# Two edits to a hybrid decoder trunk: the matmuls of two inversion levels issued together in the first mixer's recurrence, and two tiles of gate-and-up allocated in another order

## The chip, the cores and the metric

The kernel runs on one core of a Trainium2 chip. The metric is the device time of one execution in microseconds (us), the median of three runs. The engines are named as in the profile: PE does matmuls, PEld its weight loads, DVE, ACT and POOL are the vector, scalar and GpSimd engines, SP issues the DMAs. L987 is line 987 of the kernel. PSUM, into which PE writes, has banks of 128x512 float32 values.

## The reference

Two layers over 1024 tokens of width 1024, in float32. Cut to the parts that the change touches:

```python
def mixer_ab(h, ...):                     # layer 0
    qkv, z, beta_raw, alpha_raw, gate_b, gate_c, sc_in = split_cols(h @ w_in, AB_SPLITS)
    ...
    o_a = gated_delta_rule(q, k, v, g, beta)
    o_a = rms_norm(o_a, norm_g) * silu(z)
    o_b = gate_b * causal_depthwise_conv(gate_c * sc_in, sc_conv_w)
    return concatenate([o_a, o_b]) @ w_out

def gated_delta_rule(q, k, v, g, beta):   # chunkwise
    ...
    sol = triangular_solve(a_strict + eye(c), rhs, lower=True, unit_diagonal=True)
    ...                                   # then a scan over the chunks with a state per head

def swiglu(h, w_gate, w_up, w_down):      # after the mixer of each layer
    return (silu(h @ w_gate) * (h @ w_up)) @ w_down
```

The mixer of layer 1 (HGRN2 and dilated window attention) is not touched.

## The kernel before, in words

Activations lie transposed in two halves of 512 tokens. A product in float32 is made of three fp32r matmuls on split operands (`mm3`, L123 to L125): every weight tile arrives by DMA as `raw` and is split by an ACT cast (L99) and a DVE subtraction (L100) into a unit `w`.

**The recurrence of layer 0** (`delta`, in `mixer_ab`). Its 1024 tokens are eight chunks of 128. The inverse of each chunk's triangular matrix is built from 32x32 blocks in levels. `level1` and `level2` (matmuls at L971 and L987, 32x32 tiles) make the off-diagonal blocks of the 64x64 triangles; `level3` and `level4` (L999 and L1008, 64x64 tiles) make those of the 128x128 triangle. Each level writes its matmuls into one part of a PSUM bank of the kind `psg` (two buffers) and a reader takes them out: DVE L975 (`z1`), DVE L990 (a block of `yt`), ACT L1002 (`z2`), DVE L1009 (a block of `yt`). After L1009 DVE makes `y2` and `y1` (L1013, L1015). Levels of different chunks share a bank: in one step `level4` of chunk c+1 and `level2` of chunk c+2 write into `la`, in the next `level3` of chunk c+2 and `level1` of chunk c+3 write into `lb`. The columns are disjoint, but an access of one engine to a bank is ordered against another engine's access to the same bank, so matmuls into a bank wait for a reader of it that stands ahead of them in the program. Around the levels stand `values` (L1030, L1032), `state` (L1045, whose DVE part is L1049), `level5` (L1021), `outputs` (L1059, L1061) and `gated` (L1085).

`delta` is a generator. `short_conv` runs the projections of the short convolution and, after each half projection (12 matmuls of 128x512), calls `tick`, which runs `delta` up to its next `yield`. PE's order in this stage is the order of the program (`manual_schedule`); the order of DVE, ACT, POOL and SP is laid out by a planner, which starts from the program's order.

**Gate and up** (`Up`, once per layer). A product of 2x2 blocks is done with seven block products, `p1`, `p2`, `p5`, `p6`, `p7` and two in `end`, of 12 matmuls each for one of 22 column groups f. `turn` opens it while the second half's norm is still being made; there the order of PE, DVE, ACT and POOL is as written. It closes the trunk pool, which held the four 8 KB tiles a0, b0, a1, b1 (two halves by two quarters of the residual h), and opens the pool `up` over the same memory (`close()` and `self.right = right("up")`, L505 and L506). In `up` a tile takes its place in the order of first allocation: two weight units of 8 KB (`take`), four `hid` buffers of 2 KB, four kept buffers `kr` of 2 KB (`kept`), a pad. A tile waits for what last used its memory. The last uses are, in DVE's written order: a1 by the low part `t3l` (`rest(t3, a1)`), b0 by `t4l`, b1 by `b22l`; a0 last in the subtraction ahead of `t4l`. `p7` copies its bank into a kept tile (ACT L362, tile `c`) and adds another bank on DVE (L363). `end` first runs the product `a22` into the same bank as `p7` (tiles `t4h`, `t4l`), then `s4` (`b22h`, `b22l`), then DVE L372 and L377, ACT L378, POOL L379 and two DMAs.

Of the kernel before, what the change touches and what calls it, by code (L numbers as in the profile page):

```python
# [52 lines left out]
def hybrid_trunk_kernel(ctx: ExitStack, tc: tile.TileContext, x_t, w_all, w_four, w_down, w_ba, vecs, c_f, c_i, c_rope, out):  # L53
# [33 lines left out]
    def psg():  # L87
        return ps.tile([P, HT], F32, tag="g", name="psg", bufs=2)
# [160 lines left out]
    class Up:  # L249
# [160 lines left out]
        def turn(self, tr, row, b11, b21, hx, close, left, right):  # L410
# [57 lines left out]
            g = [self.snap(0)]  # L468
# [35 lines left out]
            rest(b22, b1)  # L504
            close()  # L505
            self.right = right("up")  # L506
            us = [self.take(), self.take()]
            self.first = [self.hidden()]
            self.p7(0, t3)
            self.right.tile([P, 32], F32, name="pad")  # L510
            self.p7(1, t3)
            self.add11(1, g[1])
# [111 lines left out]
    def mixer_ab(hn, rb, hp, close):  # L624
# [15 lines left out]
        with ExitStack() as es:  # L640
# [309 lines left out]
            def delta(yd, xd, load_al, load_cx):  # L950
# [4 lines left out]
                def hb(ap):  # L955
                    return ap[:, :, None].to_broadcast([P, 4, P])

                def bt(tag, shape=None, bufs=2):
                    return bp.tile([P] + (shape or [4, P]), F32, tag=tag, name=tag, bufs=bufs)
# [4 lines left out]
                ys, y2s, z1s, z2s, wts, us, sts, os_all, uu = {}, {}, {}, {}, {}, {}, {0: None}, {}, {}  # L964


                def level1(c, lv):
                    yt, x64, e0 = yts[c % 2], x64s[c % 2], c * 4
                    for h in range(4):
                        for r in (0, 64):  # L970
                            T.matmul(lv[r:r + 32, h * 32:(h + 1) * 32], als[c][r + 32:r + 64, h, r:r + 32],  # L971
                                     yd[r + 32:r + 64, e0 + h, :], start=True, stop=True)
                    z1 = z1s[c] = bt("z1", [4, 32])
                    for r in (0, 64):
                        V.tensor_copy(z1[r:r + 32], lv[r:r + 32, 0:P].rearrange("p (h t) -> p h t", h=4))  # L975
                    for b in range(4):
                        G.tensor_copy(yt[b * 32:(b + 1) * 32, :, b * 32:(b + 1) * 32],
                                      yd[b * 32:(b + 1) * 32, e0:e0 + 4, :])
                    for b in range(2):
                        G.tensor_copy(x64[b * 32:(b + 1) * 32, :, b * 32:(b + 1) * 32],  # L980
                                      xd[b * 32:(b + 1) * 32, e0:e0 + 4, :])

                def level2(c, lv):
                    yt, x64, z1 = yts[c % 2], x64s[c % 2], z1s.pop(c)
                    for h in range(4):
                        for r in (0, 64):
                            T.matmul(lv[r:r + 32, 256 + h * 32:256 + (h + 1) * 32], xd[r:r + 32, c * 4 + h, :],  # L987
                                     z1[r:r + 32, h, :], start=True, stop=True)
                    for r in (0, 64):
                        V.tensor_scalar(yt[r:r + 32, :, r + 32:r + 64],  # L990
                                        lv[r:r + 32, 256:256 + P].rearrange("p (h t) -> p h t", h=4),
                                        -1.0, None, op0=MULT)
                    for h in range(4):
                        V.transpose(x64[32:64, h, 0:32], yt[0:32, h, 32:64])

                def level3(c, lv):
                    al, yt = als.pop(c), yts[c % 2]
                    for h in range(4):
                        T.matmul(lv[0:64, 256 + h * 64:256 + (h + 1) * 64], al[64:128, h, 0:64],  # L999
                                 yt[64:128, h, 64:128], start=True, stop=True)  # L1000
                    z2 = z2s[c] = bp.tile([64, 4, 64], F32, tag="z2", name="z2", bufs=1)
                    S.copy(z2, lv[0:64, 256:512].rearrange("p (h t) -> p h t", h=4))  # L1002
                    load_al(c + 3)

                def level4(c, lv):
                    yt, x64, z2 = yts[c % 2], x64s[c % 2], z2s.pop(c)
                    for h in range(4):
                        T.matmul(lv[0:64, h * 64:(h + 1) * 64], x64[:, h, :], z2[:, h, :], start=True, stop=True)  # L1008
                    V.tensor_scalar(yt[0:64, :, 64:128], lv[0:64, 0:256].rearrange("p (h t) -> p h t", h=4),  # L1009
                                    -1.0, None, op0=MULT)  # L1010
                    if c:
                        y2 = y2s[c] = bt("y2", bufs=1)
                        V.tensor_tensor(y2, yt, hb(sca["c2"][:, c, :]), op=MULT)  # L1013
                    ys[c] = bt("y1")
                    V.tensor_tensor(ys[c], yt, hb(sca["c1"][:, c, :]), op=MULT)  # L1015

                def level5(c):
                    cx, y2 = cxs[c], y2s.pop(c)
                    o = psg()
                    for h in range(4):  # L1020
                        T.matmul(o[:, h * P:(h + 1) * P], cx[:, h, 0:P], y2[:, h, :], start=True, stop=True)  # L1021
                    wts[c] = bt("wt")
                    S.copy(wts[c], v4(o))

                def values(c):

                    cx, sp_ = cxs[c], sts[c]
                    pu = psm()
                    for h in range(4):
                        T.matmul(pu[:, h * P:(h + 1) * P], ys[c][:, h, :], cx[:, h, P:2 * P], start=True, stop=c == 0)  # L1030
                        if c:
                            T.matmul(pu[:, h * P:(h + 1) * P], wts[c][:, h, :], sp_[:, h, :], start=False, stop=True)  # L1032
                    u2 = None
                    if c < 7:
                        u2 = bt("u2", bufs=1)
                        V.tensor_tensor(u2, v4(pu), hb(sca["cu"][:, c, :]), op=MULT)
                    u = bt("u", bufs=1)
                    S.copy(u, v4(pu))
                    uu[c] = u, u2

                def state(c):
                    cx, sp_, u2 = cxs[c], sts[c], uu[c][1]
                    p2 = psm()
                    for h in range(4):
                        T.matmul(p2[:, h * P:(h + 1) * P], cx[:, h, 0:P], u2[:, h, :], start=True, stop=True)  # L1045
                    sn = sts[c + 1] = bt("st")
                    if c:
                        for h in range(4):
                            V.scalar_tensor_tensor(sn[:, h, :], sp_[:, h, :], sca["gt"][:, c, h:h + 1],  # L1049
                                                   p2[:, h * P:(h + 1) * P], op0=MULT, op1=ADD)  # L1050
                    else:
                        V.tensor_copy(sn, v4(p2))
# [17 lines left out]
                def gated(c):  # L1070
# [18 lines left out]
                    V.scalar_tensor_tensor(go, v4(o), vec[:, R_DNG:R_DNG + 1], szc, op0=MULT, op1=MULT)  # L1089
                    dma(catd[half][0:4, :, cc * P:(cc + 1) * P].rearrange("k p t -> p k t"), go)  # L1090

                for c in range(-3, 8):
                    if c > -3:
                        if c >= 0:
                            values(c)
                        la = psg() if c < 7 else None
                        if 0 <= c + 1 < 8:
                            level4(c + 1, la)
                        if 0 <= c + 2 < 8:
                            level2(c + 2, la)  # L1100
                        yield
                    if 0 <= c < 7:
                        state(c)
                    lb = psg() if c < 6 else None
                    if 0 <= c + 2 < 8:
                        level3(c + 2, lb)
                    if 0 <= c + 3 < 8:
                        level1(c + 3, lb)
                    if 1 <= c + 1 < 8:
                        level5(c + 1)  # L1110
                    if c >= 0:
                        outputs(c)
                    if c >= 1:
                        gated(c - 1)
                    yield
# [3 lines left out]
            def small():  # L1119

                yield
                step(8, 0)
                for _ in range(3):
                    yield
                parts = inverses()
                for _ in range(21):
                    yield
                yield from delta(*parts)
# [521 lines left out]
    for half in range(NH):  # L1650
        hn.append([quarter(), quarter()])
        for d in range(KT):
            x, g = tr.at(half, d), vec[:, R_MIX + d:R_MIX + d + 1]
# [165 lines left out]
```

## Time and profile before

| | |
|---|---|
| median of three runs | 2687.57 us (2687.46 to 2688.88) |
| profiled execution, its own time | 2687.8 us |
| its span, first to last instruction | 2686.0 us |
| mean granted TensorE clock | 0.996 |
| PE busy | 2654.1 us (99%) |
| DVE, ACT, POOL busy | 1479.6, 986.0, 480.4 us |
| recurrence with its levels | about 305 to 434 us |
| `turn` of gate and up | about 525 to 587 us in layer 0, 1999 to 2061 us in layer 1 |

A timeline row gives the start, the length, the engine and line, the operation, output<-inputs, the shapes and the number of instructions merged. A bracket at the end is the idle time of the engine before it and who ended it. Matmuls overlap: one of 128x512 is shown 0.39 us long, and the next starts 0.23 us after it. A row of the view of waits gives the total, the times and the longest in us. A row of the view by windows gives the length, then busy time and instructions of PE, PEld, DVE, ACT and POOL, then the granted clock, the DMA share and GB/s.

### The profile page before, as it was taken

To read this page: it belongs to the slowest core of one execution; us is meant where nothing else is said; L and a number is where in the kernel's file an instruction comes from. 1 tells how busy PE (TensorE), PEld (TensorE's weight loads), DVE (VectorE), ACT (ScalarE), POOL (GpSimd) and SP (SyncE) were. 2 spreads that over 40 slices of the span, in tenths; PEclk is the share of its full clock that TensorE was granted. 3 is DMA by queue.
4 is the path that set the end of the run, shared out by engine and by line. 5 is a ranking of instruction groups with operands and counts; after the bars stand their busy time and mean duration, and the time that the engine had idled before them with its cause. 6 is when DMAs were issued, how large, how long until landed. Compare 5 with 4: busy or idle time off the path is not lost.

```text
span 2686.0 us, 36890 instructions
## 1 busy us (share of the span) xinstructions
PE 2654.1 (99%) x14604; PEld 2221.7 (83%) x14604; DVE 1479.6 (55%) x2463; ACT 986.0 (37%) x1623; POOL 480.4 (18%) x434
## 2 busy tenths in 40 slices
PE   8999999999999999999999999999999999999998
PEld 6888788878888888888888888888887888888887
DVE  7887676583434443345665557477658344444342
ACT  4432123343333332323444345354434333333232
POOL 0110121334333201010000000000034343320100
PEclk9999999999999999999999999999999999999999
DMA  3424346422222384441222322323742222237342
GB/s 131 141 96 165 108 140 208 146 75 90 84 81 81 99 274 129 154 131 52 79 67 73 87 64 68 99 64 123 241 147 75 91 86 81 91 101 262 114 137 94
DMA packets 166285, 310.65 MB, mean 116 GB/s; under 512 B 26048, under 2 KB 65504, under 8 KB 165984
## 3 DMA queue, kind: packets, MB, share of 16 engines
q1 hardware_dynamic: 166112, 308.30, 35.3%
q8 instruction: 114, 1.87, 0.3%
q14 instruction: 59, 0.48, 0.1%
HBM read 234.22 MB, written 74.01 MB: 115 GB/s over the span
## 4 chain that ended last, share of the span: by engine, by line
PE 94%; DVE 3%; issue 1%; DMA 1%; ACT 1%; POOL 0%; SPq 0%; POOLq 0%; DVEq 0%; ACTq 0%
PE psu L123 20%; PE psu L125 20%; PE psu L124 20%; PE psg L123 5%; PE psg L125 5%; PE psg L124 5%; PE psm L123 3%; PE psm L124 3%; PE psm L125 3%; PE psm L1487 1%; PE psm L1461 1%; PE psg L1250 1%; PE psm L195 1%; PE psm L1476 1%; DVE h L413 1%
## 5 line engine op out<-in xcount | busy, mean ns | idle before, releaser
L100 DVE TENSOR_TENSOR w<-raw,w 128x1024 fp32r<-128x1024 f32 (+1 forms) x324 | 404.8, 1251 | 442.5 <-ACT w L99 441.2
L99 ACT CAST w<-raw 128x1024 fp32r<-128x1024 f32 (+1 forms) x324 | 319.5, 987 | 635.2 <-PE psg L125 230.8
L123 PE MATMUL psu<-hnh,w 128*128 128x512 f32 x1328 | 530.2, 399 | 6.9 <-ACT w L99 6.9
L125 PE MATMUL psu<-hnh,w 128*128 128x512 f32 x1328 | 520.3, 392 | 0.0
L124 PE MATMUL psu<-hnl,w 128*128 128x512 f32 x1328 | 518.6, 391 | 0.0
L123 PEld LDWEIGHTS psu<-hnh,w 128*128 128x128 f32 x1328 | 250.7, 189 | 57.4 <-ACT w L99 6.9
L125 PEld LDWEIGHTS psu<-hnh,w 128*128 128x128 f32 x1328 | 250.1, 188 | 54.1 <-DVE w L100 0.8
L124 PEld LDWEIGHTS psu<-hnl,w 128*128 128x128 f32 x1328 | 250.6, 189 | 49.6 <-DVE hnl L1656 0.2
L183 POOL TENSOR_TENSOR acc<-acc,sq 128x512 f32<-128x512 f32 x48 | 73.0, 1520 | 531.2 <-ACT sq L179 426.3
L123 PE MATMUL psu<-hidq,w 128*128 128x512 f32 (+1 forms) x352 | 134.8, 383 | 0.0
L125 PE MATMUL psu<-hidq,w 128*128 128x512 f32 (+1 forms) x352 | 134.6, 382 | 0.0
L124 PE MATMUL psu<-hidq,w 128*128 128x512 f32 (+1 forms) x352 | 134.6, 382 | 0.0
L123 PE MATMUL psu<-w,hnh 128*128 128x512 f32 (+1 forms) x320 | 113.1, 353 | 0.0
L125 PE MATMUL psu<-w,hnl 128*128 128x512 f32 (+1 forms) x320 | 111.2, 347 | 0.0
L124 PE MATMUL psu<-w,hnh 128*128 128x512 f32 (+1 forms) x320 | 111.1, 347 | 0.0
L337 DVE TENSOR_TENSOR gt<-gt,psm 128x512 f32<-128x512 f32 x40 | 27.5, 688 | 145.2 <-PE psm L125 142.8
L379 POOL TENSOR_TENSOR hid<-hid,c 128x512 f32<-128x512 f32 x44 | 83.2, 1891 | 127.6 <-ACT hid L378 127.6
L305 POOL TENSOR_TENSOR raw<-raw,ws 128x512 f32<-128x512 f32 x38 | 51.4, 1354 | 281.8 <-DVE w L100 281.8
L1288 POOL COPY attn<-ac 32x128 f32<-32x128 f32 x32 | 13.4, 418 | 434.4 <-DVE ac L1254 381.6
L100 DVE TENSOR_TENSOR hidq<-hr,hidq 128x1024 fp32r<-128x1024 f32 x44 | 54.2, 1231 | 49.6 <-ACT hidq L99 48.9
L125 PEld LDWEIGHTS psu<-hidq,w 128*128 128x128 f32 x352 | 66.2, 188 | 12.9
L124 PEld LDWEIGHTS psu<-hidq,w 128*128 128x128 f32 x352 | 66.2, 188 | 12.9
(420 smaller groups left out, 5665.6 us busy)
## 6 DMA issues: line engine op xcount, KB each, us to landing
raw<-in_dram SPq DMA_DIRECT2D x274, 512.0 KB, 3.6
hid<-hid SPq DMA_DIRECT2D x88, 256.0 KB, 2.2
hr<-hid SPq DMA_DIRECT2D x44, 512.0 KB, 4.5
hd<-h SPq DMA_DIRECT2D x48, 256.0 KB, 2.7
h<-hd SPq DMA_DIRECT2D x48, 256.0 KB, 6.0
scr_c<-cx SPq DMA_DIRECT2D x8, 1216.0 KB, 5.1
h<-in_dram SPq DMA_DIRECT2D x32, 256.0 KB, 5.4
cxb<-scr_c SPq DMA_DIRECT2D x8, 1024.0 KB, 5.9
```

The costliest lines, as they stand in the source:

```text
L99: S.copy(hi, src)
L100: eng.tensor_tensor(lo, src, hi.bitcast(F32), op=SUB)
L123: T.matmul(o, lh, rh, start=first and i == 0, stop=False, **kw)
L124: T.matmul(o, lh, rl, start=False, stop=False, **kw)
L125: T.matmul(o, ll, rh, start=False, stop=last and i == n - 1, **kw)
L183: (eng or G).tensor_tensor(a, a, q, op=ADD)
L195: T.matmul(st[:, j:j + 1], x[:, j * P:(j + 1) * P], onesn, start=i + j == 0, stop=i == 1, skip_group_check=True)
L305: G.tensor_tensor(a[:, HT:], a[:, HT:], s[:, :HT], op=SUB)
L337: V.tensor_tensor(g, g, self.y.pop(f), op=ADD)
L379: G.tensor_tensor(h, h, self.c22.pop(f), op=MULT)
L413: eng.tensor_tensor(dst, x, y, op=SUB)
L1250: T.matmul(od[r * 32:(r + 1) * 32, c * 32:(c + 1) * 32], a[:, z], x[:, z], start=True, stop=True, tile_position=(0, r * 32))
```

## The change

In each level a bare `yield` is put between its matmuls and its reader, which makes the level a generator. A new function `levels` takes the two levels of a step, runs the matmuls of both, and then the readers of both, in the old order among themselves:

```diff
                         for r in (0, 64):
                             T.matmul(lv[r:r + 32, h * 32:(h + 1) * 32], als[c][r + 32:r + 64, h, r:r + 32],
                                      yd[r + 32:r + 64, e0 + h, :], start=True, stop=True)
+                    yield
                     z1 = z1s[c] = bt("z1", [4, 32])
...
+                def levels(*fs):
+
+                    fs = [(f, c) for f, c in fs if 0 <= c < 8]
+                    if fs:
+                        o = psg()
+                        gs = [f(c, o) for f, c in fs]
+                        for _ in range(2):
+                            for g in gs:
+                                next(g, None)
+
                 for c in range(-3, 8):
                     if c > -3:
                         if c >= 0:
                             values(c)
-                        la = psg() if c < 7 else None
-                        if 0 <= c + 1 < 8:
-                            level4(c + 1, la)
-                        if 0 <= c + 2 < 8:
-                            level2(c + 2, la)
+                        levels((level4, c + 1), (level2, c + 2))
                         yield
                     if 0 <= c < 7:
                         state(c)
-                    lb = psg() if c < 6 else None
-                    if 0 <= c + 2 < 8:
-                        level3(c + 2, lb)
-                    if 0 <= c + 3 < 8:
-                        level1(c + 3, lb)
+                    levels((level3, c + 2), (level1, c + 3))
```

In `turn` the second added unit is taken after `p7(0)`, so that the pool `up` is laid out as unit, `hid`, `kr`, unit, pad instead of unit, unit, `hid`, `kr`, pad:

```diff
             self.right = right("up")
-            us = [self.take(), self.take()]
+            us = [self.take()]
             self.first = [self.hidden()]
             self.p7(0, t3)
+            us.append(self.take())
             self.right.tile([P, 32], F32, name="pad")
             self.p7(1, t3)
```

No instruction is added or removed.

## The prediction on record

> **What bounds the kernel now.** I read the page first, for the engine that sets the end.
>
> ```profile
> PE 2654.1 (99%) x14604; PEld 2221.7 (83%) x14604; DVE 1479.6 (55%) x2463; ACT 986.0 (37%) x1623; POOL 480.4 (18%) x434
> PE 94%; DVE 3%; issue 1%; DMA 1%; ACT 1%; POOL 0%; SPq 0%; POOLq 0%; DVEq 0%; ACTq 0%
> ```
>
> PE is busy 99% of the span and is 94% of the chain that ended last. So time is won only where PE stands idle or runs slowly, and off-PE work costs nothing until PE waits for it. Next the view of waits for PE, over the whole run, without the one wait at the start:
>
> ```profile
> PE psu L123 <- ACT c L362: 5.1, 2, 2.5
> PE psg L987 <- DVE yt L1009: 4.1, 7, 1.0
> PE psg L971 <- ACT z L1002: 3.5, 7, 0.5
> ```
>
> These three rows are what the two edits aim at: two waits in gate and up (one per layer), and fourteen short ones in the recurrence. Last, windows over these places, for the granted clock (the number after the POOL column):
>
> ```profile
> 305.00:434.00 129.00, 121.39 (x1036) 105.74 (x1036) 86.56 (x214) 27.27 (x46) 20.41 (x48) 1.00 0.39 122
> 574.40:579.00 4.60, 4.60 (x13) 3.69 (x14) 2.77 (x5) 4.57 (x7) 0.00 (x0) 0.63 0.00 0
> 2048.00:2053.00 5.00, 5.00 (x15) 3.96 (x16) 3.16 (x5) 4.97 (x8) 0.00 (x0) 0.66 0.00 0
> ```
>
> The recurrence runs at clock 1.00. Behind each of the two gate-and-up waits PE gets only 0.63 and 0.66 for some 5 us, which the view of waits doesn't show.
>
> **Part one: the recurrence.** Nothing is added; a wait goes from between two groups of matmuls. PE's timeline gives the price, from the start of the first group of a pair to the start of the second: first and last of the seven pairs L999/L971, first and last of the seven L1008/L987, then each first group where no second follows.
>
> ```profile
> 311.63 0.68 PE L999 MATMUL psg<-yt,al 64*64 64x64 f32 x8
> 312.76 0.44 PE L971 MATMUL psg<-yd,al 32*32 32x32 f32 x16 [0.46 <-ACT z L1002]
> ...
> 390.81 0.68 PE L999 MATMUL psg<-yt,al 64*64 64x64 f32 x8
> 392.00 0.44 PE L971 MATMUL psg<-yd,al 32*32 32x32 f32 x16 [0.51 <-ACT z L1002]
> ...
> 316.10 0.67 PE L1008 MATMUL psg<-z,x 64*64 64x64 f32 x8
> 317.28 0.44 PE L987 MATMUL psg<-z,xd 32*32 32x32 f32 x16 [0.51 <-DVE yt L1009]
> ...
> 400.69 0.67 PE L1008 MATMUL psg<-z,x 64*64 64x64 f32 x8
> 402.33 0.44 PE L987 MATMUL psg<-z,xd 32*32 32x32 f32 x16 [0.97 <-DVE yt L1009]
> ...
> 406.58 0.67 PE L999 MATMUL psg<-yt,al 64*64 64x64 f32 x8
> 407.19 0.38 PE L1021 MATMUL psg<-y,cxb 128*128 128x128 f32 x1
> ...
> 415.52 0.67 PE L1008 MATMUL psg<-z,x 64*64 64x64 f32 x8
> 416.12 0.50 PE L123 MATMUL psu<-hnh,w 128*128 128x512 f32 x1
> ```
>
> L999 to L971 takes 1.13 first and 1.19 last, 8.24 over the seven. L1008 to L987 takes 1.18 first and 1.64 last, 8.80 over the seven. Without a wait the first group costs 0.61 and 0.60. No row shows L971 or L987 right behind such a group, so this handover is an estimate. Its low end is 0.51: the group's 0.67 less one matmul's shown length of some 0.22, plus 0.06 of spacing. Its high end is 0.67 and a little, the group's full length. I take 0.605, the two rows of the same groups. The gain is 8.24 + 8.80 - 14 x 0.605 = 8.6 us; the ends give 9.9 and 7.7.
>
> A rule of the skill bears on this estimate. The Trainium skill, "TensorE: Matmul & The Clock Gate", Part 3, says that a weight load overlaps matmuls in flight only when its row group differs. L1008 uses rows 0 to 63 and L987 starts on rows 0 to 31, so by the rule those seven handovers would cost 0.67 and the gain would be 0.5 us less; in L999/L971 the groups differ. No run shown here has these two groups back to back.
>
> What becomes late? The readers now stand behind both groups, and their results are wanted earlier. The tightest is the block of `yt` from L990, which L999 reads in the next step:
>
> ```profile
> 355.60 0.41 DVE L1009 TENSOR_SCALAR yt<-psg 64x256 f32<-64x256 f32 x1
> 357.74 0.59 DVE L990 TENSOR_SCALAR yt<-psg 32x128 f32<-32x128 f32 x2
> 360.28 0.67 PE L999 MATMUL psg<-yt,al 64*64 64x64 f32 x8
> ```
>
> L990 ends at 358.33, 1.95 us ahead of L999. L999 comes 0.6 us sooner. Its L1008 started at 354.88 in the same timeline; L987 would follow at 355.49 and end at 355.93, so L1009 starts about 0.35 us later and pushes L1013, L1015 and L990. Some 1.0 us is left. `y2` (L1013) is wanted by L1021 later still, `z1` and `z2` only a step later. On the queues: DVE and ACT keep the order of their readers; `load_al` on SP is issued behind L1002 as before, which waits longer by L971's 0.4 us, and is wanted two chunks later. I cost these at nothing. If DVE's cover is gone, each further 1 us comes back once per chunk, seven times.
>
> **Part two: gate and up.** PE's, ACT's and DVE's timelines in layer 0, and PE's same wait in layer 1:
>
> ```profile
> 571.47 0.39 PE L125 MATMUL psu<-t3h,w 128*128 128x512 f32 x1
> 574.39 0.50 PE L123 MATMUL psu<-t4h,w 128*128 128x512 f32 x1 [2.52 <-ACT c L362]
> ...
> 578.82 0.40 PE L123 MATMUL psm<-b22h,w 128*128 128x512 f32 x1
> ```
> ```profile
> 570.01 0.57 ACT L357 COPY u<-psu 128x512 f32<-128x512 f32 x1
> 573.75 1.07 ACT L362 COPY c<-psu 128x512 f32<-128x512 f32 x2 [3.16 <-DVE b22l L413]
> ```
> ```profile
> 563.20 2.42 DVE L413 TENSOR_TENSOR t3l<-h,t3h 128x1024 fp32r<-128x1024 f32 x2
> ...
> 568.94 2.43 DVE L413 TENSOR_TENSOR t4l<-h,t4h 128x1024 fp32r<-128x1024 f32 x2
> 571.28 2.35 DVE L413 TENSOR_TENSOR b22l<-h,b22h 128x1024 fp32r<-128x1024 f32 x2
> 574.37 1.29 DVE L363 TENSOR_TENSOR c<-c,psm 128x512 f32<-128x512 f32 x2 [0.73 <-ACT c L362]
> ...
> 578.77 1.23 DVE L277 TENSOR_TENSOR w<-raw,w 128x1024 fp32r<-128x1024 f32 x1 [0.26 <-ACT w L276]
> ```
> ```profile
> 2047.97 0.50 PE L123 MATMUL psu<-t4h,w 128*128 128x512 f32 x1 [2.53 <-ACT c L362]
> ```
>
> The copy of the kept tile `c` waits for `b22l`, the last reader of b1: so `kr` lies on b1. That fits a pool laid out in order: the two units on a0 and b0, `hid` on a1, `kr` on b1. After the change `hid` lies on b0, `kr` on a1 and the second unit on b1. The last reader of a1 is `t3l`, done at 565.62. The first copy can then follow L357 on ACT, at 570.6, and end at 571.2, before PE comes to `t4h` at 571.70 (0.23 behind the last matmul).
>
> The price: the gap is 2.92 - 0.23 = 2.69 us. The 12 matmuls from 574.39 to 578.82 take 4.43 instead of 12 x 0.227 = 2.72, so the low clock costs 1.71 (by the window: 4.60 x 0.37 = 1.70). Layer 1 has the same idle time (2.53 against 2.52), and 5.00 x 0.34 = 1.70. Together 4.4 per layer, 8.8 us.
>
> What is late next: `t4l` is ready at 571.37, in time. `s4` needs `b22l` (573.63) and L363's first add behind it on DVE, to 574.28; PE comes to it at 574.42. The second unit (L277) ends at 580.00 even if it doesn't move and is wanted at 582.6; the first, ahead of it on DVE, is done before 578.77 and wanted at 579.87. The second unit now waits for b1, free at 573.63, long before its copy. `hid` is first written behind PE's `a22`, long after 571.37. These margins are thin (0.1 us) but hold.
>
> Further on PE reaches f = 4 some 4.4 us sooner. The next view is DVE's two L100 of that f in each layer's timeline, and PE's `p1(4)`:
>
> ```profile
> 602.41 1.22 DVE L100 TENSOR_TENSOR w<-raw,w 128x1024 fp32r<-128x1024 f32 x1
> 604.14 2.01 DVE L100 TENSOR_TENSOR w<-raw,w 128x1024 fp32r<-128x1024 f32 x1
> 608.76 0.39 PE L123 MATMUL psu<-hnh,w 128*128 128x512 f32 x1
> ...
> 2076.77 2.01 DVE L100 TENSOR_TENSOR w<-raw,w 128x1024 fp32r<-128x1024 f32 x1
> 2082.36 0.39 PE L123 MATMUL psu<-hnh,w 128*128 128x512 f32 x1
> ```
>
> PE would want the first unit at 604.36 and 2077.96. If that unit is the first L100 it is there at 603.63. If it is the second, and nothing ahead of it moves, it comes at 606.15 and 2078.78: a stall of 1.8 + 0.8 = 2.6 us. The program splits that unit first, and the chain to it also starts about 1 us sooner (L277 stands behind ACT copies that move). I take 0.3 of 0 to 2.6.
>
> **The sum.** 8.6 + 8.8 - 0.3 = 17.1 us. The profiled execution's own time is 2687.8, its span 2686.0; it lies 0.2 above the median. 2687.8 - 17.1 = 2670.7 by its clock, 2670.5 as a median. All behind these places is PE work that moves up whole.
>
> **The rivals.**
>
> *A wait takes the place of the one removed.* The weights of f = 4 are late by the full 2.6 us: 2670.5 + 2.3 = 2672.8. For it: DVE's second L100 is slow and has little lead. Against: the order of the splits.
>
> *The low clock has another cause and stays.* Then the gaps go but 2 x 1.7 us stay: 2673.9. Against it: in the windows both stretches follow the gap at once, and the recurrence with its fourteen short waits has 1.00. The Trainium skill, "TensorE: Matmul & The Clock Gate", in its table of why this matters, warns only of idle gaps above some 3 us between bursts. By that rule a gap of 2.7 us wouldn't lower the clock, and this rival's time follows. The trace disagrees so far: 0.63 and 0.66 stand behind 2.7 us.
>
> *One part does nothing.* If `kr` doesn't come to lie on a1, part two is lost: 2687.6 - 8.6 = 2679.0. If PE then waits elsewhere for each reader, part one is lost: 2679.1. For it: thin margins at `t4l` and L363. If both fail, 2687.6.
>
> *Slower.* DVE's order in the recurrence is laid out anew, and splits of weights come ahead of L990 there. The page has their price:
>
> ```profile
> L100 DVE TENSOR_TENSOR w<-raw,w 128x1024 fp32r<-128x1024 f32 (+1 forms) x324 | 404.8, 1251 | 442.5 <-ACT w L99 441.2
> ```
>
> With n splits ahead, L999 waits n x 1.25 - 1.0 us in each of seven chunks. Three give 7 x 2.75 = 19.3 us, more than the gain: 2689.8. Four give 28 us: 2698.5. It decides from three. Against it: between L1009 and L990 of the chunk quoted, DVE runs three instructions of `gated` and `level4` and no split, and the change keeps the readers' order in the program.
>
> **How the numbers follow.** Forecast 0.68; late weights at f = 4 0.10; clock stays low 0.05; one part lost 0.09; no effect 0.03; slower 0.05. About 0.2% (5.4 us) is what a measurement of this kernel can tell from no change. The first four lie below 2682.2: faster 0.92, same 0.03, slower 0.05. The range takes the handover's ends (1.3 down, 0.9 up), the 2.6 us at f = 4 and the clock rival, and about 1 us for margins I couldn't see: 2668.0 to 2676.0. It leaves out 0.17.
>
> **What would show it.** Right: no waits of PE at L987 and L971, and a first group followed by the second in about 0.6 us; L362 directly behind L357; `t4h` 0.23 us behind `t3h`; clock 1.00 there in both layers. Wrong: new PE waits at L999 for L990, at L123 for L100 near f = 4, or at `s4` for L363; L362 waiting for another reader; DVE's order changed in the recurrence.

## The result, and the profile after

The changed kernel takes 2675.41 us, the median of five runs (2674.49 to 2676.71), against 2688.56 us (2687.46 to 2689.14) for five runs of the kernel before: a ratio of 0.9953 with a 95% interval of 0.9938 to 0.9967, so 13.15 us less. The forecast was 2670.5 us. The profiled execution has 2676.71 us by its own time and a span of 2674.9 us; against the profiled one of before (2687.8 us) that is 11.1 us less.

On the changed kernel's page PE still sets the end, the first line with the engines and the second with the chain that ended last:

```profile
PE 2651.3 (99%) x14604; PEld 2219.1 (83%) x14604; DVE 1478.5 (55%) x2463; ACT 985.3 (37%) x1623; POOL 480.7 (18%) x434
...
PE 93%; DVE 3%; DMA 1%; issue 1%; ACT 0%; POOL 0%; SPq 0%; DVEq 0%; POOLq 0%; ACTq 0%
```

The changed kernel's view of waits of PE, again without the one at the start:

```profile
PE psu L123 <- ACT u L357: 3.1, 2, 2.1
...
PE psg L123 <- DVE hid L377: 0.6, 1, 0.6
PE psu L123 <- ACT c L362: 0.5, 2, 0.3
```

The fourteen waits of the recurrence are gone (7.6 us before). The two waits for L362 shrank from 5.1 to 0.5 us. But there are two new ones, 3.1 us in all, for the copy L357. (The matmuls of the levels now stand at L972, L989, L1002 and L1012, one to four lines lower; the lines of gate and up ahead of L500 are the same.)

The next view is the changed kernel's windows: over the recurrence, over the old place of the low clock in layer 0, and over the places of the new waits in layers 0 and 1. The clock is the number after the POOL column.

```profile
305.00:425.00 120.00, 120.00 (x1020) 105.24 (x1019) 85.97 (x214) 27.14 (x46) 19.42 (x48) 1.00 0.42 129
564.00:569.00 5.00, 5.00 (x24) 4.14 (x23) 3.53 (x6) 4.00 (x7) 0.00 (x0) 1.00 0.00 0
593.00:600.00 7.00, 4.87 (x15) 3.77 (x15) 4.64 (x4) 1.85 (x4) 5.10 (x3) 0.76 0.15 57
...
2066.00:2075.00 9.00, 8.08 (x36) 6.37 (x35) 6.15 (x6) 3.06 (x6) 5.13 (x3) 1.00 0.19 64
```

PE has no idle time left in the recurrence, and the clock behind `t4h` is 1.00 instead of 0.63. It is low in a new place, 593 to 600 us.

Where the 11.1 us came from, by the starts of the same matmuls in the two profiled executions; a plus is time won between this place and the one above:

| up to | before, us | after, us | won, us |
|---|---|---|---|
| first 64x64 group of the recurrence | 311.63 | 310.90 | +0.73 |
| L195 behind the first mixer | 494.77 | 485.57 | +8.47 |
| layer 0: last `t3h` ahead of `t4h` | 571.47 | 562.24 | +0.03 |
| layer 0: last matmul of `p5(3)` | 605.81 | 592.72 | +3.86 |
| layer 0: second matmul of `p1(4)` | 608.99 | 599.92 | -4.02 |
| L195 behind layer 0 | 1087.92 | 1079.77 | -0.92 |
| L195 behind the mixer of layer 1 | 1968.35 | 1960.57 | -0.37 |
| layer 1: last `t3h` ahead of `t4h` | 2045.05 | 2037.23 | +0.04 |
| layer 1: last matmul of `p5(3)` | 2079.41 | 2067.73 | +3.86 |
| layer 1: first matmul of `p1(4)` | 2082.36 | 2071.91 | -1.23 |
| L195 behind layer 1 | 2561.83 | 2551.25 | +0.13 |
| end of the span | 2686.0 | 2674.9 | +0.52 |

The two edits brought 8.47 and 3.86 twice, as forecast to within 0.6 us each. Then 4.02 and 1.23 us were given back at `p7(3)`, some 30 us behind the place of the edit. PE's timeline of the changed kernel there, layer 0 and then layer 1:

```profile
592.72 0.39 PE L125 MATMUL psg<-t1h,w 128*128 128x512 f32 x1
595.24 0.50 PE L123 MATMUL psu<-t3h,w 128*128 128x512 f32 x1 [2.13 <-ACT u L357]
...
597.40 0.63 PE L124 MATMUL psu<-t3l,w 128*128 128x512 f32 x1
...
599.92 0.39 PE L124 MATMUL psu<-hnl,w 128*128 128x512 f32 x1
...
2069.04 0.50 PE L123 MATMUL psu<-t3h,w 128*128 128x512 f32 x1 [0.92 <-ACT u L357]
```

From 592.72 to 595.24 PE loses 2.29 us (2.52 less one step of 0.23). The 13 steps to 599.92 take 4.68 us instead of 2.95, so a low clock costs 1.73 more; before the change the same 14 steps took 3.18 us (605.81 to 608.99). In layer 1 the wait is 0.92 us and the clock stays at 1.00.

Why is a copy on ACT late, an engine that is busy 37% of the span? ACT's timeline of the changed kernel shows what stands ahead of it, DVE's, POOL's and SP's what stands ahead of that:

```profile
589.41 1.05 ACT L99 CAST w<-ws 128x1024 fp32r<-128x1024 f32 x1 [7.36 <-POOL ws L291]
590.37 0.63 ACT L340 ACTIVATE gt<-gt 128x512 f32<-128x512 f32 x1
590.90 1.99 ACT L99 CAST w<-raw 128x1024 fp32r<-128x1024 f32 x2
594.08 0.63 ACT L378 ACTIVATE hid<-hid 128x512 f32<-128x512 f32 x1 [1.20 <-DVE hid L377]
594.62 0.57 ACT L357 COPY u<-psu 128x512 f32<-128x512 f32 x1
```
```profile
592.24 1.22 DVE L100 TENSOR_TENSOR w<-raw,w 128x1024 fp32r<-128x1024 f32 x1
593.37 0.68 DVE L377 TENSOR_TENSOR hid<-u,psg 128x512 f32<-128x512 f32 x1
```
```profile
588.09 1.29 POOL L291 TENSOR_TENSOR ws<-ws,raw 128x512 f32<-128x512 f32 x1 [3.73 <-DMA raw<-in_dram]
```
```profile
583.09 1.75 SPq L263 DMA_DIRECT2D raw<-in_dram  x2
```

L357 has its input by about 590.4 us, when `p6(3)` ends: it waits for its turn in ACT's queue. The first cast shown of that queue is a weight cast of f = 4, which had waited 7.36 us for a sum on POOL, and that one 3.73 us for a transfer of raw weights issued at 583.09. (On SP this issue came at once behind the DMA L380 at 582.68, which had waited for POOL's L379.) Right ahead of L357 stands L378. It waits for DVE's L377, and L377 stands in DVE's queue behind the split (L100) of the same weights. Before the change the same chain ran from 599.58 to 604.80, the same 5.2 us long. So the chain moved up by 10.2 us and PE by 13.09 us. Before the change the copy had ended at 605.37, 0.67 us ahead of PE.

### The profile page after: what moved, and what is told of

It is laid out like the page before. It is cut to its first block, busy times and chain, and to the rows that moved or that the text cites. A ratio compares the mean times of both kernels' runs of the same rounds, so it can differ in the third digit from the quotient of the medians.

```text
span 2674.9 us, 36882 instructions
## 1 busy us (share of the span) xinstructions
PE 2651.3 (99%) x14604; PEld 2219.1 (83%) x14604; DVE 1478.5 (55%) x2463; ACT 985.3 (37%) x1623; POOL 480.7 (18%) x434
## 4 chain that ended last, share of the span: by engine, by line
PE 93%; DVE 3%; DMA 1%; issue 1%; ACT 0%; POOL 0%; SPq 0%; DVEq 0%; POOLq 0%; ACTq 0%
PE psu L123 20%; PE psu L125 20%; PE psu L124 20%; PE psg L123 5%; PE psg L124 5%; PE psg L125 5%; PE psm L124 3%; PE psm L123 3%; PE psm L125 3%; PE psm L1494 1%; PE psm L1468 1%; DMA raw<-in_dram 1%; PE psg L1257 1%; PE psm L1483 1%; DVE h L413 1%
## 5 line engine op out<-in xcount | busy, mean ns | idle before, releaser
L100 DVE TENSOR_TENSOR w<-raw,w 128x1024 fp32r<-128x1024 f32 (+1 forms) x324 | 404.2, 1250 | 435.3 <-ACT w L99 434.3
L379 POOL TENSOR_TENSOR hid<-hid,c 128x512 f32<-128x512 f32 x44 | 84.1, 1911 | 125.9 <-ACT hid L378 125.9
L100 DVE TENSOR_TENSOR hidq<-hr,hidq 128x1024 fp32r<-128x1024 f32 x44 | 53.9, 1225 | 52.0 <-ACT hidq L99 51.3
```

The lines of the kernel that those rows point to most:

```text
L100: eng.tensor_tensor(lo, src, hi.bitcast(F32), op=SUB)
L379: G.tensor_tensor(h, h, self.c22.pop(f), op=MULT)
```

## The experiments

Six kernels were run, the first four beside the kernel before at 2688.84 us, the last two beside it at 2687.70 us. For the first four the theory taken from the trace is that the two edits work as predicted, with two amendments: the new wait at `p7(3)` comes from turn's own order (the splits for the added units stand behind the gates on DVE, so the raw buffer and all that follows it is late); and the short wait left at `t4h` comes from the pad of 128 bytes, which puts the kept tiles off a1. The rivals are that one of the edits, or the lead that the recurrence won, disturbs the other's stage, and that the wait left at `t4h` has another cause than the pad. The last two kernels were made for what the third showed unexpectedly, the rate of the matmuls: the theory is that the places of the two weight units in the pool set it. Each expectation names the theories that it sets against each other; in the later ones, `e3_pad` is the kernel with the pad ahead of the tiles, and `e5_order` the one with the splits ahead of the gates.

**The recurrence alone.** The changed kernel with the second edit undone:

```diff
-            us = [self.take()]
+            us = [self.take(), self.take()]
             self.first = [self.hidden()]
             self.p7(0, t3)
-            us.append(self.take())
```

> The recurrence edit alone; gate and up as before. Theory (the gate-and-up edit moves PE's wait from t4h to p7(3), because the weights of f = 4 don't come sooner): 8.5 us less than before, 2680.0 us; PE waits 2.5 us for L362 in each layer with a low clock behind it, and not at all for L357. Rival (the recurrence edit upset the planner's order in gate and up): PE waits for L357 here too, and the time is 2682 to 2684.

It measured 2679.44 us (2678.09 to 2680.05), ratio 0.9964 (0.9952 to 0.9977): 9.4 us less than before. Its view of waits of PE:

```profile
PE psu L123 <- ACT c L362: 5.2, 3, 2.6
...
PE psu L123 <- ACT u L357: 0.2, 1, 0.2
```

The old wait is there again in both layers, and of the new one 0.2 us is left. So PE's earlier arrival by 8 us, which this edit brings, isn't what makes the long wait for L357. One thing came otherwise than expected: a low clock stands behind the old wait in layer 1 only. This kernel's windows behind the wait, layer 0 and then layer 1:

```profile
566.87:571.87 5.00, 5.00 (x22) 4.11 (x23) 3.16 (x5) 4.97 (x8) 0.00 (x0) 1.00 0.00 0
2039.80:2044.80 5.00, 4.99 (x15) 4.06 (x16) 3.17 (x5) 4.97 (x8) 0.00 (x0) 0.66 0.00 0
```

In the profiled execution, 8.3 us shorter than that of before by its span, the recurrence brought 7.97 us and the low clock that didn't come in layer 0 another 1.54; some 0.5 us were lost at `p7(3)` of layer 0. So the 9.4 us aren't the recurrence's alone.

**The order of the tiles alone.** The kernel before with the second edit only (the reverse of the diff above).

> The gate-and-up edit alone; the recurrence as before. Theory (the wait moves): 3.9 us won per layer at t4h, 4.0 lost again in layer 0 and 1.1 in layer 1 at p7(3), where PE waits for L357; about 2685.8 us. Rival (the wait for L357 comes from the recurrence edit): no wait for L357, 2680.8 us.

It measured 2685.35 us (2682.13 to 2687.61), ratio 0.9985 (0.9976 to 0.9994): 3.5 us less. With the 9.4 that makes 12.9 of the 13.15 us by medians. PE's waits in this kernel, and its timeline at `p7(3)` of layer 0:

```profile
PE psu L123 <- ACT u L357: 2.1, 2, 1.2
PE psg L1000 <- DVE yt L991: 1.4, 1, 1.4
...
PE psu L123 <- ACT c L362: 0.5, 2, 0.3
```
```profile
604.74 0.50 PE L123 MATMUL psu<-t3h,w 128*128 128x512 f32 x1 [1.25 <-ACT u L357]
605.07 0.39 PE L124 MATMUL psu<-t3l,w 128*128 128x512 f32 x1
605.30 0.39 PE L125 MATMUL psu<-t3h,w 128*128 128x512 f32 x1
```

The wait for L357 is there without the first edit: it belongs to the second. It is 1.25 and 0.90 us here, and in layer 0 shorter than the 2.13 of the changed kernel; the matmuls behind it are 0.23 us apart, so no low clock follows. Its length goes with that of one transfer. From the issue of the raw weights (SP L263) to POOL's sum of them (L291) it took 4.12 us here in layer 0 and 3.77 in layer 1, and 5.00 and 3.80 in the changed kernel; in all four cases PE's wait is 2.87 or 2.88 us less than that. Why the transfer took longest in layer 0 of the changed kernel isn't shown.

That the time came within 0.5 us of the expected 2685.8, and that the two medians add up so well, is in part luck. In the profiled execution only 1.55 us were lost at `p7(3)` of layer 0, where 4.0 had been expected, but 1.37 us in the recurrence, where nothing had: PE waited there once at L1000 (L999 of the kernel before) for L991, because an instruction ahead of it on DVE had waited 3.18 us for a DMA.

**The pad ahead of the tiles.** The pool has to end where it did, so the pad moves to its start, and the kept tiles fall exactly on a1:

```diff
             self.right = right("up")
+            self.right.tile([P, 32], F32, name="pad")
             us = [self.take()]
             self.first = [self.hidden()]
             self.p7(0, t3)
             us.append(self.take())
-            self.right.tile([P, 32], F32, name="pad")
```

> The changed kernel with the 128-byte pad of the pool allocated first instead of behind the second unit. Theory (the pad at the end shifts the pool by 128 bytes, so that the first kept tile lies over the last bytes of b0 as well as on a1, and waits for t4l): with the pad first L362 follows L357 on ACT at once, the 0.3 us wait at t4h goes in both layers (0.45 us each with its restart), but the wait for L357 at p7(3) grows by as much in layer 0; total within 0.6 us of 2675.4. Rival (kr lies on b0 altogether, or L362 waits for something else that ends with t4l): nothing changes at t4h.

Its ACT timeline has the first L362 directly behind L357:

```profile
561.45 0.58 ACT L357 COPY u<-psu 128x512 f32<-128x512 f32 x1
561.93 0.59 ACT L362 COPY c<-psu 128x512 f32<-128x512 f32 x1
```

and PE's waits for it at `t4h` are gone. In the changed kernel the same ACT view has

```profile
560.82 0.58 ACT L357 COPY u<-psu 128x512 f32<-128x512 f32 x1
562.26 1.07 ACT L362 COPY c<-psu 128x512 f32<-128x512 f32 x2 [0.86 <-DVE t4l L413]
```

so the copy waited for `t4l`, the last reader of b0, and not for `t3l` as predicted. That settles the layout: 128 bytes of the first kept tile lay on b0. The wait for L357 didn't grow, as had been expected: it is 1.96 and 0.98 us. But the time is 2682.70 us (2681.52 to 2683.96), ratio 0.9978 (0.9969 to 0.9987): 7.3 us longer than the changed kernel, where at most a fraction of a microsecond was expected. The windows over 100 us of the loop over f, without any wait of PE in them, show where; first this kernel, then the changed one:

```profile
700.00:800.00 100.00, 100.00 (x439) 82.08 (x438) 42.42 (x43) 35.28 (x48) 36.46 (x26) 1.00 0.24 79
2200.00:2300.00 100.00, 100.00 (x438) 82.11 (x437) 41.64 (x43) 34.83 (x48) 38.23 (x28) 1.00 0.24 80
```
```profile
700.00:800.00 100.00, 100.00 (x443) 82.84 (x442) 42.87 (x44) 35.70 (x48) 36.70 (x26) 1.00 0.24 79
2200.00:2300.00 100.00, 100.00 (x443) 82.81 (x442) 40.60 (x41) 34.22 (x47) 37.41 (x27) 1.00 0.25 80
```

PE is never idle and has clock 1.00 in both, the DMA share is nearly the same, and still runs 438 matmuls where it ran 443: 1.1% fewer. Behind gate and up, from 1000 to 1075 us, both run 332. So the loss lies in the loops that read their weights from this pool. It outweighs the 0.43 us per layer that the pad's place wins at `t4h`.

**The splits ahead of the gates.** The layout of the changed kernel; in `turn` the work on the two added units goes ahead of the gates, so that DVE frees their raw buffer sooner:

```diff
             self.p7(1, t3)
-            self.add11(1, g[1])
-            self.gate11(0)
-            self.gate11(1)
             low = self.prepared(1, s, None, "s4", us[0])
             low()
             low = self.prepared(2, u2, "s3", "a22", us[1])
             low()
+            self.add11(1, g[1])
+            self.gate11(0)
+            self.gate11(1)
```

> The changed kernel with the splits of the two added units written ahead of the two gates in the turn, so that the buffer of the raw weights u2 comes free about 2 us sooner; layout as in the changed kernel. Theory (the weights of f = 4 are late because the chain of raw buffers, POOL and splits starts at these splits): PE's wait for L357 falls from 2.1 to below 1 us in layer 0, without a low clock behind it, and to 0 in layer 1; 3 to 4.5 us less, about 2671.5 us. Rival (the new layout itself holds the unit or the hid tiles back): the waits stay at 2.1 and 0.9 us, 2675 us.

It measured 2671.72 us (2671.32 to 2673.14), ratio 0.9937 (0.9925 to 0.9950). In its view of waits of PE there is no row for L357. Its ACT timeline at the same place:

```profile
585.31 1.05 ACT L99 CAST w<-ws 128x1024 fp32r<-128x1024 f32 x1 [2.22 <-POOL ws L291]
...
589.99 0.63 ACT L378 ACTIVATE hid<-hid 128x512 f32<-128x512 f32 x1 [0.46 <-DVE hid L377]
591.15 0.59 ACT L357 COPY u<-psu 128x512 f32<-128x512 f32 x1 [0.53 <-PE psu L125]
```

DVE's split of the second added unit (L277) stands at 566.66 here and at 568.40 in the changed kernel:

```profile
566.66 1.22 DVE L277 TENSOR_TENSOR w<-raw,w 128x1024 fp32r<-128x1024 f32 x1
```
```profile
568.40 1.22 DVE L277 TENSOR_TENSOR w<-raw,w 128x1024 fp32r<-128x1024 f32 x1 [0.26 <-ACT w L276]
```

1.74 us sooner there, the next raw transfers are issued on SP directly behind this split in both kernels (567.91 against 569.65), those of f = 4 at 579.82 against 583.09, the cast of f = 4 starts 4.10 us sooner, and L357 now waits for PE instead of PE for it. So the wait hung on turn's order, as the theory has it, and not on the layout, which is the same. By medians this version is 17.1 us below before and 3.7 us below the changed kernel; its runs (at most 2673.14) and the changed kernel's (at least 2674.49) don't overlap, though the intervals of the two ratios (0.9925 to 0.9950 and 0.9938 to 0.9967) do.

**Two more places for the pad**, both with the order just shown. The first puts it between `hid` and the kept tiles, so that the first unit stays 128 bytes off and the kept tiles and the second unit lie exactly on a1 and b1:

```diff
             us = [self.take()]
             self.first = [self.hidden()]
+            self.right.tile([P, 32], F32, name="pad")
             self.p7(0, t3)
             us.append(self.take())
-            self.right.tile([P, 32], F32, name="pad")
```

> The reordered turn of e5_order with the 128-byte pad placed between the hid and the kr tiles: the first unit and hid stay 128 bytes off the old tiles, kr lies exactly on a1, the second unit exactly on b1. Theory A (the slower matmuls of e3_pad come from where the two units in this pool lie, since PE reads their weights): the wait at t4h goes, 0.9 us in all, but the second unit is now where e3_pad had it, so half of e3_pad's loss of rate comes back: about 440.5 matmuls per 100 us in the gate-and-up loop instead of 443, 2674 to 2676 us. Theory B (it comes from where hid or kr or the first unit lies, or from the pool as a whole): 443 per 100 us with 2670.8 us, or 438 with 2678 us.

It measured 2677.41 us (2676.82 to 2678.13), ratio 0.9962 (0.9947 to 0.9977). Its windows have

```profile
2200.00:2300.00 100.00, 100.00 (x440) 82.38 (x439) 40.57 (x41) 33.64 (x46) 36.75 (x27) 1.00 0.25 80
```

The second leaves the pad at the end and makes it 256 bytes:

```diff
-            self.right.tile([P, 32], F32, name="pad")
+            self.right.tile([P, 64], F32, name="pad")
```

> The reordered turn of e5_order with a pad of 256 bytes at the end of the pool instead of 128, so that the whole pool lies 256 bytes off. If any shift off the other units keeps the rate, 443 matmuls per 100 us in the gate-and-up loop and 2671.7 us as e5_order. If 128 bytes is half of a spacing that counts, the rate falls to 438 as in e3_pad and the time rises to about 2679 us. The waits are those of e5_order either way.

It measured 2679.48 us (2678.27 to 2682.29), ratio 0.9969 (0.9958 to 0.9981), and its windows

```profile
2200.00:2300.00 100.00, 100.00 (x439) 82.15 (x438) 40.34 (x41) 34.13 (x47) 37.38 (x27) 1.00 0.24 77
```

With both units 128 bytes off PE runs 443 matmuls in 100 us, with one of them 440, with none, or with all 256 bytes off, 438 to 439. In the first of the two kernels L362 also follows L357 at once (562.47 behind 561.99), so the 0.43 us per layer are there to be had, but they cost more than they bring. The time, 5.7 us above the version with the new order, is a little more than was expected.

## Why the prediction was right or wrong

**The recurrence: right.** 8.6 us were forecast and 8.47 came. The handover that no row of before showed is in the changed kernel's PE timeline, one pair of each kind:

```profile
350.01 0.68 PE L1012 MATMUL psg<-z,x 64*64 64x64 f32 x8
350.62 0.44 PE L989 MATMUL psg<-z,xd 32*32 32x32 f32 x16
...
354.85 0.68 PE L1002 MATMUL psg<-yt,al 64*64 64x64 f32 x8
355.45 0.44 PE L972 MATMUL psg<-yd,al 32*32 32x32 f32 x16
```

0.61 and 0.60 us, against 0.605 taken. The rule of row groups (the Trainium skill, "TensorE: Matmul & The Clock Gate", Part 3) would have made the first 0.67; the trace shows no difference between the two pairs. The margins at `yt` and `y2` held: no wait at the 64x64 groups or at L1026. The "slower" rival fell with them, in this kernel; in the one with the second edit alone a late DMA did make PE wait for that block of `yt` once.

**Gate and up at its own place: right but for 128 bytes.** The layout was read as kept tiles on a1; the pad at the pool's end puts them 128 bytes lower, so the first copy waited for `t4l` too. The changed kernel's PE timeline:

```profile
562.24 0.39 PE L125 MATMUL psu<-t3h,w 128*128 128x512 f32 x1
562.90 0.50 PE L123 MATMUL psu<-t4h,w 128*128 128x512 f32 x1 [0.27 <-ACT c L362]
```

0.66 instead of 0.23, and 3.86 instead of 4.4 us per layer. The kernel's description named the pad; the prediction left it out of the sum of the pool's places.

**The step that failed is "Further on PE reaches f = 4 some 4.4 us sooner ... I take 0.3 of 0 to 2.6."** The term is 5.25 us (4.02 and 1.23). The weights of f = 4 were indeed late, as the first rival said, though ahead of DVE's split, which it named: the transfer and the casts came late. And the prediction looked only at the user of those weights, `p1(4)` on PE. Their casts stand in ACT's queue ahead of L357, which has nothing to do with f = 4, and PE's `p7(3)`, 12 matmuls ahead of `p1(4)`, needs the bank that L357 empties. So PE met the late transfer 2.7 us sooner than the rival priced it, and in layer 0 the clock fell again behind the wait, 1.73 us that no case of the prediction held. That the chain of weights moves only a little with PE was in the text ("about 1 us sooner"). What was left out is its way to PE through ACT and DVE, whose queues run in a fixed order. The version with the splits ahead of the gates removes the wait and reaches 2671.72 us, within 1.2 us of the forecast.

**The number owes something to luck.** The median, 2675.41 us, lies inside the range of 2668.0 to 2676.0 by 0.6 us, and the profiled execution, 2676.71 us, lies outside it. The top of the range held 2.6 us at f = 4 and 3.4 us for a low clock that stays at `t4h`. What came was 5.25 us at f = 4, and no low clock at `t4h`.

**The clock: right in this kernel, but the price isn't fixed.** The rival that the low clock stays fell: the windows behind `t4h` have 1.00 in both layers now that the gap is 0.27 us. But the prediction gave each gap of this length 1.7 us for the clock, and the recurrence alone shows one of 2.56 us with a clock of 1.00 behind it. The table of the Trainium skill's same page, which warns of idle gaps above some 3 us, doesn't fit here: the clock fell behind a gap of 2.13 us at 593 us.

**What stays open.** Two of the small rows of the table are the clock of single executions. The 0.73 us ahead of the recurrence are 1.38 won behind the first norm, less 0.65 lost ahead of it: from 33 to 40 us the granted clock was 0.57 before and 0.76 after. The 0.52 at the end are the last matmuls, L209, at 0.50 before and 0.74 after. The -0.92 between `p1(4)` and L195 of layer 0 (0.58 of it the wait for L377 in the view of waits) and the -0.37 in the mixer of layer 1 are differences of single executions too, and nothing was tried on them. The links between the raw buffer, POOL's sums and the late transfer were read from the trace; only the whole chain was moved. Why the matmuls run 1.1% slower with the units at other offsets isn't known. In the profiled executions the sum of 8.6 + 8.8 - 0.3 = 17.1 us became 8.47 + 7.72 - 5.25 + 0.16 = 11.1 us, where 0.16 is the total of all the small rows of the table. By medians the gain is 13.15 us, 2 us more: the profiled execution of the changed kernel is the longest of its five runs, 1.3 us above the median, and that of before lies 0.8 us below its own. Whether the clock fell at 593 us in the other four runs isn't known.

## What to carry to other kernels

When a stall on the bounding engine goes, ask of each in-order queue that feeds it what stands there ahead of the next result that it needs, however unrelated, and whether that head moves forward by as much; here the casts and splits of the next group's weights held up a 0.57 us copy. Before a low clock behind a gap is counted as won, look whether it stands behind such a gap every time. Lay out a pool with every pad in the sum before saying whose memory a tile waits for. And after moving weight tiles in memory, count matmuls in a window in which PE never waits, since the waits and the clock don't show a rate that fell by 1%.

## What the hardware showed that was not expected

The rate of matmuls in the loop over f depended on where in the partition the two weight units lay, with PE busy throughout and the granted clock at 1.00: 443 in 100 us with both 128 bytes off the old tiles' places, 440 with one, 438 to 439 with none or with both 256 bytes off. That is 0.226 against 0.228 us a matmul. The slower rates stand in three kernels, in both layers. The kernel before and the recurrence alone, whose two units lie 128 bytes off two other old tiles, have 443 as well. The cause was not found.

The length of an idle time of PE doesn't tell by itself whether the granted clock falls behind it. It fell behind 2.52 and 2.53 us (before), 2.53 us (the recurrence alone, layer 1) and 2.13 us (the changed kernel). It did not behind 0.92 us (the changed kernel, layer 1), 1.25 us (the tiles' order alone), 1.96 us (the pad ahead of the tiles), and not behind 2.56 us, the longest of them. That one and the one of 2.53 us stand in the same execution, the recurrence alone; its PE timeline, layer 0 and then layer 1:

```profile
566.87 0.50 PE L123 MATMUL psu<-t4h,w 128*128 128x512 f32 x1 [2.56 <-ACT c L362]
567.21 0.40 PE L124 MATMUL psu<-t4l,w 128*128 128x512 f32 x1
...
569.76 0.39 PE L123 MATMUL psm<-b22h,w 128*128 128x512 f32 x1
...
2039.81 0.80 PE L123 MATMUL psu<-t4h,w 128*128 128x512 f32 x1 [2.53 <-ACT c L362]
2040.40 0.63 PE L124 MATMUL psu<-t4l,w 128*128 128x512 f32 x1
```

The 12 matmuls of layer 0 take 2.89 us here, and took 4.43 in the kernel before, behind a gap 0.04 us shorter. Where the clock fell, steps of 0.43 us stood for some 3.4 us, and they began at once (2039.81 us here), about 0.6 us (before, layer 0), 1.3 us (the changed kernel) or 1.5 us (before, layer 1) behind PE's restart. So 2.13 us can be enough in these kernels, and 2.56 us can pass without a cost. What decides it was not found.
